# Large tiles moved to multiples of 512 bytes, and two modulation rounds summed on VectorE

## The chip, the cores and the metric

The kernel runs on 1 core of one Trainium2 chip. The metric is the device time of one execution in microseconds (us); the time before is the median of 3 runs. TensorE multiplies matrices, VectorE and ScalarE work elementwise, GpSimd (POOL in the profile) issues some small transfers, and SyncE (SP) issues the loads of the weights. Everything is float32; a product of two such matrices is made of three products in a reduced form of it (below).

## The reference

One sequence of 256 tokens with 1024 features passes through four layers: retention, forgetting attention, a convolution block with a dense feed-forward part, and a short convolution with a mixture of 8 experts. The first two are modulated by a vector c:

```python
c_act = jax.nn.silu(c)
for i in range(DEPTH):
    shift, scale, gate = jnp.split(c_act @ mod_w[i] + mod_b[i], 3, axis=-1)
    h = _rms_norm(x, norm_g[i]) * (1.0 + scale[:, None, :]) + shift[:, None, :]
    y = _retention(...) if i == 0 else _forgetting_attention(...)
    x = x + gate[:, None, :] * y
```

`mod_w` is 2 x 1024 x 3072: a vector times a matrix, of which only weight is large. In the last layer each token is sent to two of eight experts, and each expert has three matrices of 1024 x 3584:

```python
for e in range(N_EXPERTS):
    h = jax.nn.silu(x @ w_gate[e]) * (x @ w_up[e])
    out = out + gates[..., e:e + 1].astype(x.dtype) * (h @ w_down[e])
```

## The kernel before

All weights pass through one stream (class `Stream`, line 66) in units of 1 MiB: SP loads a unit into a raw buffer of 128 x 2048, ScalarE casts it into the high part wH (line 122), VectorE subtracts to get the low part wL (line 123), and TensorE multiplies with both (`mm3`, lines 229 to 233): high by high, high by low, low by high. There are three pairs of wH and wL, so a split runs at most two units ahead. In the retention there are three raw buffers; in the experts ten. `get` hands out the next unit and sends the loads and splits behind it on their way. Units of the modulation are not split: the raw buffer itself is read, and is given back once its reader is done.

The retention goes through four heads (`P_`, line 614): the products for q and k (weights stationary, 256 columns), then v and a gate (tokens stationary, 512 columns), with the attention of the head before (`A_`) in between. The modulation of layer 0's shift and scale is made in the start-up (line 1664). The rest is made in two rounds of eight steps in the heads: round 1 (the gates of both layers) in heads 0 and 1, round 2 (shift and scale of layer 1) in heads 2 and 3. `mods` (line 609) takes a step behind a projection, 2, 6, 4 and 4 times in the four heads. Step k multiplies 128 rows of `mod_w` by 128 values of c: four matmuls, each with one column of `sc` repeated 32 times as stationary side in its own quarter of the array's columns, add to one bank that is held through the round (line 499). `mod_end` (line 503) adds the bias.

The order of the work is made when the program is built: instructions are placed by priority (the order of the text) as their inputs become ready in its estimate, and each engine then works through its list in that order.

Where the tiles lie follows from their sizes. Pools are laid one behind the other, a tile is rounded up to 32 bytes per partition. In the program before, the small tiles of the pool `cp` leave the next large one (x) at byte 23680 of each partition, which is 46 x 512 + 128, and nearly everything behind it has sizes that are multiples of 512. So x, raw, wH, wL, hT, hH, hL, xn and the retention's and attention's outputs start at 128 past a multiple of 512. The statistics of the convolution block (192 bytes) put what follows in its pool (csg, cR, cW) at 320, and the router's rl, rmask and rpos (64 + 64 + 96 bytes) put what follows (oh, identR, three raw buffers, soH, soL, mh, xg, ohT, mhH, mhL) at 352. In the experts the gathered rows of expert e lie in xg where e is a multiple of 3, else in hT or hH (line 1329). ident, the first part of cst, lies at 416.

Of the kernel before, what the change touches and what calls it, by code (L numbers as in the profile page):

```python
# [6 lines left out]
F32 = mybir.dt.float32  # L7
# [3 lines left out]
ALU = mybir.AluOpType  # L11
# [3 lines left out]
P = 128  # L15
DM = 1024
# [9 lines left out]
C_STRIU, C_IOTA, C_TIE, C_ID32, C_MAIN = 146, 274, 530, 594, 626  # L26
# [166 lines left out]
class Kern:  # L193
# [4 lines left out]
    def t(self, pool, shape, tag, dt=F32, bufs=None):  # L198
        self.uid += 1
        kw = {} if bufs is None else {"bufs": bufs}  # L200
        return pool.tile(shape, dt, tag=tag, name=f"{tag}_{self.uid}", **kw)
# [228 lines left out]
    def setup(self, tmp):  # L430
        nc, a = self.nc, self.a
        cp = self.cp
        cv = cp.tile([P, 8], F32, name="cv")
        nc.scalar.dma_start(out=cv, in_=a["c"].rearrange("o (p k) -> p (o k)", k=8))
        self.x = self.t(self.xp, [P, 2, DM], "x", bufs=2)
        self.c = c = cp.tile([P, C_MAIN], F32, name="cst")
        nc.scalar.dma_start(out=c[:, 0:C_EARLY], in_=a["cst"][:, 0:C_EARLY])
        self.ident = c[:, C_ID:C_ID + P]
        vn = tmp.tile([32, P], F32, name="vn")
        nc.scalar.dma_start(out=vn[0:16, :], in_=a["norm_g"].rearrange("i d -> (i d)").rearrange("(k p) -> k p", p=P))  # L440
        nc.scalar.dma_start(out=vn[16:32, :], in_=a["mod_b"][0, 0:2 * DM].rearrange("(k p) -> k p", p=P))
        self.sc = cp.tile([P, 8], F32, name="sc")
        nc.scalar.activation(self.sc, cv, AF.Silu)
        self.ones = cp.tile([P, P], F32, name="ones")
        nc.gpsimd.memset(self.ones, 1.0)
        self.vr = [tmp.tile([P, P], F32, name=f"vr{i}") for i in range(2)]
        for r in self.vr:
            nc.gpsimd.memset(r, 1.0)
        self.wr = cp.tile([P, 8, N_EXP], F32, name="wr")
        ps = self.acc()  # L450
        nc.tensor.transpose(ps[:, 0:32], vn, self.ident[0:32, 0:32])
        self.vn = cp.tile([P, 32], F32, name="vnT")
        nc.vector.tensor_copy(self.vn[:, 0:24], ps[:, 0:24])
        nc.vector.tensor_scalar(self.vn[:, 24:32], ps[:, 24:32], 1.0, None, op0=ALU.add)
# [15 lines left out]
    def vectors(self):  # L470

        ps = self.acc()
        for i, r in enumerate(self.vr):
            self.nc.tensor.transpose(ps[:, i * P:(i + 1) * P], r, self.ident)
        self.v = self.cp.tile([P, 2 * P], F32, name="v")
        self.nc.vector.tensor_copy(self.v, ps[:, 0:2 * P])

    def vec(self, name):
        o = self.vcol[name]
# [6 lines left out]
    def mod_start(self, parts):  # L486

        b = self.t(self.bp, [P, 512], "mbias", bufs=1)
        for q, (i, n0) in enumerate(parts):
            self.nc.gpsimd.dma_start(out=b[32 * q:32 * (q + 1), :],  # L490
                                     in_=self.a["mod_b"][i, n0:n0 + 512].partition_broadcast(32))
        self.mps, self.mbias, self.mk = self.acc(), b, 0

    def mod_step(self):
        k = self.mk
        raw = self.st.get("mod")
        s = self.sc[:, k:k + 1].to_broadcast([P, 32])
        for q in range(4):
            self.nc.tensor.matmul(self.mps[32 * q:32 * (q + 1), :], s, raw[:, q * 512:(q + 1) * 512],
                                  start=(k == 0), stop=(k == 7), tile_position=(0, 32 * q))  # L500
        self.mk += 1

    def mod_end(self, tag):
        m = self.t(self.bp, [P, 512], tag, bufs=1)
        self.nc.vector.tensor_tensor(m, self.mps, self.mbias, op=ALU.add)
        return m

    def shift_scale(self, m, i):
# [243 lines left out]
    def fox(self):  # L752
        nc = self.nc
        fT, hH, hL = self.hT, self.hH, self.hL
        c = self.c
        with self.tc.tile_pool(name="fox", bufs=1) as fp:
# [82 lines left out]
                    nc.scalar.copy(v[:, tt, :], ps[tt])  # L839
                return v  # L840

            gq, gk = self.v[0:66, P + 24:P + 25], self.v[0:66, P + 25:P + 26]

            def stage_t(d):

# [87 lines left out]
            with self.soon():  # L933
                self.xo = self.t(self.xp, [P, 2, DM], "x", bufs=2)
                self.new_h(False)
                for tt in range(2):
                    r = self.residual(acc, grow, tt)
                    for nh in range(2):
                        xo = self.xo[:, tt, nh * 512:nh * 512 + 512]
                        if self.dbg:  # L940
                            self.dump_part("x2", xo, tt, nh)
                        nc.vector.scalar_tensor_tensor(xo, xo, r[:, 0:1], g[:, nh * 512:nh * 512 + 512],
                                                       op0=ALU.mult, op1=ALU.mult)
# [91 lines left out]
    def conformer(self):  # L1035
        nc = self.nc
        hH, hL = self.hH, self.hL
        with self.tc.tile_pool(name="conf", bufs=1) as cp:
# [4 lines left out]
            def glu(u):  # L1043
                sg = self.t(cp, [P, 512], "csg", bufs=2)

                def gate(ps):
                    nc.scalar.activation(sg, ps, AF.Sigmoid)
                    if u == 3:
                        self.table(AF.Silu, sg[:, 0:1])

                ps = self.proj_two("cg", "ca", u == 0, gate)
                if u == 0:
                    v = self.t(self.hp, [P, 2, DM], "xn", bufs=1)[:, :, 0:30 + T]
                    nc.gpsimd.memset(v[:, :, 0:30], 0.0)
                    nc.vector.tensor_tensor(v[:, :, 30:30 + T], sg.rearrange("p (c t) -> p c t", c=2),
                                            ps.rearrange("p (c t) -> p c t", c=2), op=ALU.mult)
                    return v
                nc.vector.tensor_tensor(sg, sg, ps, op=ALU.mult)
                R = self.t(cp, [P, 8 * (32 + T)], "cR", bufs=3).rearrange("p (q c t) -> p q c t", q=4, c=2)
                nc.gpsimd.memset(R[:, :, :, 0:36], 0.0)  # L1060
                sv = sg.rearrange("p (c t) -> p c t", c=2)
                for q in range(4):
                    for tau in range(4):
                        d, x = R[32 * tau:32 * (tau + 1), q, :, 32 + tau:32 + T], sv[32 * q:32 * (q + 1), :, 0:T - tau]
                        if q == tau:
                            nc.scalar.copy(d, x)
                        else:
                            (nc.gpsimd if (q + tau) % 2 else nc.sync).dma_start(out=d, in_=x)
                return R
# [26 lines left out]
                    turn(k)  # L1096
                stats(u)

            st = self.t(cp, [P, 2, 4, 6], "cst", bufs=1)

            def stats(u):
                for tt in range(2):
# [17 lines left out]
            v = glu(0)  # L1120
# [16 lines left out]
            with self.soon():  # L1137
                xn = self.t(self.hp, [P, 2, DM], "xn", bufs=1)
# [9 lines left out]
                for tt in range(2):  # L1148
                    nc.vector.tensor_scalar(xn[:, tt, 0:512], accT[tt][0], mv[:, tt, 0:1], r[:, tt:tt + 1],
                                            op0=ALU.subtract, op1=ALU.mult)  # L1150
# [37 lines left out]
    def short_conv(self):  # L1188
        nc = self.nc
        hH, hL = self.hH, self.hL  # L1190
        with self.tc.tile_pool(name="sc", bufs=1) as sp:
            oH = sp.tile([P, 8, T], F32R, name="soH")
            oL = sp.tile([P, 8, T], F32R, name="soL")
            wv = self.v[:, P:P + 24].rearrange("p (j k) -> p j k", j=3)
            xs = None
            v = lambda u: xs[:, u % 2 * 516:u % 2 * 516 + 516].rearrange("p (c t) -> p c t", c=2)
            for u in range(4):
                if u == 0:
                    def conv_in(ps):
                        nonlocal xs  # L1200
                        xs = self.t(self.hp, [P, 2, DM], "xn", bufs=1).rearrange("p a n -> p (a n)")
                        nc.gpsimd.memset(xs[:, 0:2 * 516], 0.0)
                        gate(ps)

                def gate(ps):
                    nc.scalar.copy(v(u)[:, :, 2:T + 2], ps.rearrange("p (c t) -> p c t", c=2))

                ps = self.proj_two("sc", "sh", u == 0, gate if u else conv_in)
                vu = v(u)
                nc.vector.tensor_tensor(vu[:, :, 2:T + 2], vu[:, :, 2:T + 2], ps.rearrange("p (c t) -> p c t", c=2), op=ALU.mult)  # L1210
                y = xs[:, 1032:1544].rearrange("p (c t) -> p c t", c=2)
                for ch in range(2):
                    k = 2 * u + ch
                    nc.vector.tensor_scalar(y[:, ch, :], vu[:, ch, 0:T], wv[:, 0, k:k + 1], None, op0=ALU.mult)
                    for j in (1, 2):
                        nc.vector.scalar_tensor_tensor(y[:, ch, :], vu[:, ch, j:j + T], wv[:, j, k:k + 1], y[:, ch, :],
                                                       op0=ALU.mult, op1=ALU.add)
                ps = self.proj_wst("sb", hH, hL)
                nc.vector.tensor_tensor(y, y, ps.rearrange("p (c t) -> p c t", c=2), op=ALU.mult)
                self.split_to(oH[:, 2 * u:2 * u + 2, :], oL[:, 2 * u:2 * u + 2, :], y, "dve")  # L1220
            return self.out_proj("so", oH, oL)


    def router_tiles(self, pool):
        t = lambda n, *sh: pool.tile([P, *sh], F32, name=n)
        self.rl = t("rl", 2, 8)
        self.rt = t("rmask", 2, 8), t("rpos", 3, 8)
        self.oh = self.t(pool, [P, 2, 2, P], "oh", F32R, bufs=1)

# [557 lines left out]
```

## Time and profile before

| | us |
|---|---|
| median of 3 runs (lowest to highest) | 1857.95 (1856.32 to 1862.34) |
| the profiled execution, its time | 1857.9 |
| the profiled execution, span of its instructions | 1856.1 |
| TensorE busy in the span | 1804.0 |
| VectorE busy | 1412.2 |
| ScalarE busy | 1063.9 |

The span runs from the first instruction to the last; busy time is a sum over very different stages, so the stages are read apart. The start-up takes the first 60 us, the retention goes on to about 260, the attention to about 450, the convolution block and its feed-forward part to about 710, the short convolution to about 830, and the experts to the end. PE is TensorE's multiplication and PEld its loading of the stationary side; DVE is VectorE, ACT ScalarE.

### The profile page before, as it was taken

Reading aid. Unit: us, or ns where it says so; the run is one execution under the profiler, and the core shown is the slowest. Engines: PE = TensorE matmul, PEld = TensorE weight load, DVE = VectorE, ACT = ScalarE, POOL = GpSimd, SP = SyncE. Lnnn points to the kernel's source line nnn. Section 1 sums busy time; section 2 is a strip of 40 time slices with the busy share of each in tenths; the row PEclk is TensorE's granted clock in tenths of the full one; section 3 lists DMA queues with packets and bytes.
Section 4 is the critical chain, followed back from the end, with each engine's and each line's share of the span. In section 5 each row is a group of like instructions: output and inputs, shape, how many; then the busy total and the mean of one; then the engine's idle time right before and its main releaser. Section 6 shows DMA issues by size and latency. Waiting matters only on the chain. (4 is left out here: it accounts for less than half of the span.)

```text
span 1856.1 us, 24359 instructions
## 1 busy us (share of the span) xinstructions
PE 1804.0 (97%) x9741; PEld 1485.4 (80%) x9741; DVE 1412.2 (76%) x1469; ACT 1063.9 (57%) x1036; POOL 65.7 (4%) x112
## 2 busy tenths in 40 slices
PE   6999999999999999999999999999999999999996
PEld 3867778788789998987888878878878888788785
DVE  2755656657875556778889888888888888888887
ACT  2333444664353333437777776767767767777674
POOL 1000002000200000000000000000000000000000
PEclk8999999999999999999999999999999999999998
DMA  9677636327546556647999999999999999999991
GB/s 358 213 263 270 216 125 207 114 86 240 159 134 199 189 182 204 228 159 260 351 367 348 354 339 349 374 351 357 338 346 364 375 353 347 341 356 363 362 360 74
DMA packets 252615, 509.34 MB, mean 274 GB/s; under 512 B 12347, under 2 KB 68782, under 8 KB 251470
## 3 DMA queue, kind: packets, MB, share of 16 engines
q1 hardware_dynamic: 249550, 500.64, 76.7%
q0 software_dynamic: 2592, 6.97, 1.2%
q8 instruction: 78, 1.28, 0.3%
q14 instruction: 43, 0.35, 0.1%
q10 hardware_dynamic: 352, 0.10, 0.0%
HBM read 504.28 MB, written 1.05 MB: 272 GB/s over the span
## 5 line engine op out<-in xcount | busy, mean ns | idle before, releaser
L123 DVE TENSOR_TENSOR wL<-raw,wH 128x2048 fp32r<-128x2048 f32 (+2 forms) x582 | 1032.3, 1800 | 229.3 <-ACT wH L122 227.9
L122 ACT CAST wH<-raw 128x2048 fp32r<-128x2048 f32 (+2 forms) x582 | 869.6, 1518 | 427.7 <-PE mm L232 118.2
L231 PE MATMUL mm<-hH,wH 128*128 128x256 f32 x816 | 232.2, 285 | 0.0
L232 PE MATMUL mm<-hL,wH 128*128 128x256 f32 x816 | 231.6, 284 | 0.0
L233 PE MATMUL mm<-hH,wL 128*128 128x256 f32 x816 | 231.2, 283 | 0.2 <-DVE wL L123 0.2
L231 PE MATMUL mm<-wH,hH 128*128 128x512 f32 (+1 forms) x512 | 200.1, 392 | 3.1 <-ACT wH L122 2.6
L232 PE MATMUL mm<-wL,hH 128*128 128x512 f32 (+1 forms) x512 | 199.6, 390 | 2.9 <-DVE wL L123 2.9
L232 PE MATMUL acc<-wL,mhH 128*128 128x512 f32 x448 | 179.1, 400 | 0.0
L233 PE MATMUL acc<-wH,mhL 128*128 128x512 f32 x448 | 176.6, 394 | 0.0
L231 PE MATMUL acc<-wH,mhH 128*128 128x512 f32 x448 | 164.4, 395 | 0.0
L231 PEld LDWEIGHTS mm<-hH,wH 128*128 128x128 f32 x816 | 156.5, 192 | 5.4 <-ACT wH L122 2.5
L233 PEld LDWEIGHTS mm<-hH,wL 128*128 128x128 f32 x816 | 156.5, 192 | 1.3 <-DVE wL L123 1.2
L232 PEld LDWEIGHTS mm<-hL,wH 128*128 128x128 f32 x816 | 156.5, 192 | 0.6 <-issue 0.2
L232 PE MATMUL mm<-wL,hT 128*128 128x512 f32 x336 | 131.9, 393 | 1.8 <-DVE wL L123 1.8
L232 PE MATMUL mm<-wL,xg 128*128 128x512 f32 x328 | 130.5, 398 | 1.3 <-DVE wL L123 1.2
L231 PE MATMUL mm<-wH,hT 128*128 128x512 f32 x336 | 131.5, 391 | 0.0
L233 PE MATMUL mm<-wH,hT 128*128 128x512 f32 x336 | 131.0, 390 | 0.0
L231 PE MATMUL mm<-wH,xg 128*128 128x512 f32 x328 | 130.2, 397 | 0.0
L233 PE MATMUL mm<-wH,xg 128*128 128x512 f32 x328 | 129.5, 395 | 0.0
L231 PEld LDWEIGHTS mm<-wH,hH 128*128 128x128 f32 x512 | 98.5, 193 | 28.5 <-ACT wH L122 4.5
L232 PEld LDWEIGHTS mm<-wL,hH 128*128 128x128 f32 x512 | 98.2, 192 | 25.0 <-DVE wL L123 6.4
L233 PE MATMUL mm<-wH,hL 128*128 128x512 f32 (+1 forms) x288 | 111.4, 387 | 0.7 <-DVE hL L361 0.7
(376 smaller groups left out, 2422.3 us busy)
## 6 DMA issues: line engine op xcount, KB each, us to landing
raw<-in_moe_w_gate_dram SPq DMA_DIRECT2D x112, 1024.0 KB
raw<-in_moe_w_up_dram SPq DMA_DIRECT2D x112, 1024.0 KB
raw<-in_moe_w_down_dram SPq DMA_DIRECT2D x111, 1024.0 KB
raw<-in_ret_w_in_dram SPq DMA_DIRECT2D x24, 1024.0 KB
raw<-in_mod_w_dram SPq DMA_DIRECT2D x32, 512.0 KB
raw<-in_fox_w_in_dram SPq DMA_DIRECT2D x16, 1024.0 KB
raw<-in_sc_w_in_dram SPq DMA_DIRECT2D x12, 1024.0 KB
raw<-in_ffn_w_gate_dram SPq DMA_DIRECT2D x11, 1024.0 KB
```

Of the source, the lines that this page charges most:

```text
L122: ops = (K.nc.scalar.copy(H[:, s], raw[:, s]), K.nc.vector.tensor_tensor(L[:, s], raw[:, s], H[:, s], op=ALU.subtract))
L123: K.nc.vector.tensor_tensor(L[:, s], raw[:, s], H[:, s], op=ALU.subtract))
L231: self.mm_first = mmul(ps, sH, mH, start=first, stop=False)
L232: mmul(ps, sH, mL, start=False, stop=False)
L233: self.mm_last = mmul(ps, sL, mH, start=False, stop=last)
```

## The change

Tiles are widened or narrowed so that the large ones move. In `cp`, cv takes 128 bytes for 32, cst 2560 for 2528, and v 256 for 1024, as only the 58 columns in use are kept (readers of v get the new column numbers). That is 640 bytes less, so x starts at 23040 = 45 x 512, and with it everything that was at 128 starts at a multiple of 512. The convolution block's statistics take 512 bytes for 192, and a tile rpad of 288 bytes fills up the router's 224, so that what was at 320 and 352 starts at a multiple of 512 too.

A step of the later modulation rounds is no longer four matmuls but one instruction of VectorE over 128 x 2048: the raw unit times one value per partition, in the first step written to a sum `msum`, in the others added to it. `msum` lies in the tile xn, which is free in the retention. `mod_end` sums over the partitions with four matmuls whose stationary side is ones, one per quarter, and then adds the bias as before. The bank is taken in `mod_end` and no longer at the start of the round. The start-up's modulation stays as it is.

```diff
     def setup(self, tmp):
-        cv = cp.tile([P, 8], F32, name="cv")
+        cv = cp.tile([P, 32], F32, name="cv")[:, 0:8]
...
-        self.c = c = cp.tile([P, C_MAIN], F32, name="cst")
+        self.c = c = cp.tile([P, 640], F32, name="cst")[:, 0:C_MAIN]
...
-        self.v = self.cp.tile([P, 2 * P], F32, name="v")
-        self.nc.vector.tensor_copy(self.v, ps[:, 0:2 * P])
+        self.v = self.cp.tile([P, 2 * P // 4], F32, name="v")
+        self.nc.vector.tensor_copy(self.v.rearrange("p (i n) -> p i n", i=2),
+                                   ps[:, 0:2 * P].rearrange("p (i n) -> p i n", i=2)[:, :, 0:32])
...
-        self.mps, self.mbias, self.mk = self.acc(), b, 0
+        self.mbias, self.mk = b, 0
+        self.msum = self.t(self.hp, [P, 2, DM], "xn", bufs=1).rearrange("p a n -> p (a n)")
 
     def mod_step(self):
         k = self.mk
         raw = self.st.get("mod")
-        s = self.sc[:, k:k + 1].to_broadcast([P, 32])
-        for q in range(4):
-            self.nc.tensor.matmul(self.mps[32 * q:32 * (q + 1), :], s, raw[:, q * 512:(q + 1) * 512],
-                                  start=(k == 0), stop=(k == 7), tile_position=(0, 32 * q))
+        w, o = self.sc[:, k:k + 1], self.msum
+        if k:
+            self.nc.vector.scalar_tensor_tensor(o, raw, w, o, op0=ALU.mult, op1=ALU.add)
+        else:
+            self.nc.vector.tensor_scalar(o, raw, w, None, op0=ALU.mult)
         self.mk += 1
 
     def mod_end(self, tag):
         m = self.t(self.bp, [P, 512], tag, bufs=1)
-        self.nc.vector.tensor_tensor(m, self.mps, self.mbias, op=ALU.add)
+        mps = self.acc()
+        for q in range(4):
+            self.nc.tensor.matmul(mps[32 * q:32 * (q + 1), :], self.ones[:, 0:32], self.msum[:, q * 512:(q + 1) * 512],
+                                  start=True, stop=True, tile_position=(0, 32 * q))
+        self.nc.vector.tensor_tensor(m, mps, self.mbias, op=ALU.add)
         return m
...
-            st = self.t(cp, [P, 2, 4, 6], "cst", bufs=1)
+            st = self.t(cp, [P, 128], "cst", bufs=1)[:, 0:48].rearrange("p (a b c) -> p a b c", a=2, b=4)
...
         self.rl = t("rl", 2, 8)
+        t("rpad", 72)
```

## Rows read from the trace of the kernel before

**Rows 1.** Busy time of each engine in four stretches, clock, DMA share, GB/s.
```profile
core 0: us, PE busy (x) PEld busy (x) DVE busy (x) ACT busy (x) POOL busy (x), PEclk, DMA share, GB/s
0.00:50.00 50.00, 33.75 (x205) 19.81 (x206) 16.46 (x35) 14.69 (x24) 7.38 (x19) 0.86 1.01 358
59.50:122.20 62.70, 62.70 (x376) 45.69 (x374) 38.72 (x64) 20.15 (x25) 1.11 (x2) 1.00 0.67 235
122.20:210.70 88.50, 87.78 (x494) 66.56 (x494) 54.07 (x72) 32.00 (x38) 4.24 (x8) 1.00 0.78 272
920.00:1820.00 900.00, 895.13 (x4030) 728.29 (x4029) 784.61 (x488) 645.34 (x457) 1.10 (x2) 1.00 0.98 352
```
**Rows 2.** Waits in 59.5 to 210.7 us: us in total, times, longest.
```profile
ACT wH L122 <- DMA raw<-in_ret_w_in_dram: 56.4, 12, 7.0
DVE wL L123 <- ACT wH L122: 40.0, 15, 6.4
...
PEld mm L231 <- ACT wH L122: 4.2, 5, 0.8
...
PEld mm L231 <- ACT roH L358: 1.7, 2, 0.8
```
**Rows 3.** Waits of SP's queue in the same stretch.
```profile
SPq L209 <- DVE wL L123: 48.8, 18, 4.6
SPq L209 <- PE acc L499: 45.8, 12, 5.8
```
**Rows 4.** Timeline of SP's queue in round 1: start, duration.
```profile
98.24 0.38 SPq L209 DMA_DIRECT2D raw<-in_ret_w_in_dram  x1
...
107.50 0.38 SPq L209 DMA_DIRECT2D raw<-in_ret_w_in_dram  x1
```
**Rows 5.** Timeline of TensorE around one modulation step.
```profile
65.16 0.28 PE L233 MATMUL mm<-hH,wL 128*128 128x256 f32 x1
65.36 1.06 PE L499 MATMUL acc<-raw,sc 128*32 128x512 f32 x8
...
66.58 0.28 PE L232 MATMUL mm<-hL,wH 128*128 128x256 f32 x1
```
**Rows 6.** Groups of instructions in 50 to 260 us: busy us, mean ns.
```profile
L499 PE MATMUL acc<-raw,sc 128*32 128x512 f32 x128 | 21.2, 604 | 0.0
```
**Rows 7.** Groups of VectorE's instructions in the whole span, by shape.
```profile
L123 DVE TENSOR_TENSOR wL<-raw,wH 128x2048 fp32r<-128x2048 f32 x320 | 725.2, 2288 | 76.9 <-ACT wH L122 75.7
L1378 DVE TENSOR_TENSOR mh<-mh,mm 128x512 f32<-128x512 f32 x56 | 38.4, 685 | 29.9 <-PE mm L233 29.0 <-ACT mh L1470 0.9
L1446 DVE SCALAR_TENSOR_TENSOR x<-mm,rgate,x 128x512 f32<-128x512 f32 x32 | 23.0, 746 | 9.4 <-PE mm L1438 9.4
L1696 DVE TENSOR_SCALAR xn<-x,rstd 128x1024 f32<-128x1024 f32 x2 | 1.5, 754 | 1.4 <-POOL rstd L369 1.4
L1529 DVE TENSOR_SCALAR x<-x 128x2048 f32<-128x2048 f32 x1 | 1.2, 1219 | 0.0
```
**Rows 8.** Timeline of TensorE, first and last of 12 matmuls of a down product.
```profile
892.63 0.39 PE L231 MATMUL acc<-wH,mhH 128*128 128x512 f32 x1
...
895.20 0.39 PE L233 MATMUL acc<-wH,mhL 128*128 128x512 f32 x1
```
**Rows 9.** Timeline of TensorE, first and last of 19 matmuls with xg.
```profile
896.80 0.39 PE L232 MATMUL mm<-wL,xg 128*128 128x512 f32 x1
...
901.00 0.39 PE L232 MATMUL mm<-wL,xg 128*128 128x512 f32 x1
```
**Rows 10.** Timeline of TensorE, first and last of 16 matmuls with hT.
```profile
1002.43 0.39 PE L233 MATMUL mm<-wH,hT 128*128 128x512 f32 x1
...
1005.83 0.39 PE L233 MATMUL mm<-wH,hT 128*128 128x512 f32 x1
```
**Rows 11.** Groups of TensorE's instructions from 820 us on.
```profile
L232 PE MATMUL acc<-wL,mhH 128*128 128x512 f32 x448 | 179.1, 400 | 0.0
...
L232 PE MATMUL mm<-wL,xg 128*128 128x512 f32 x328 | 130.5, 398 | 1.3 <-DVE wL L123 1.2
```
**Rows 12.** Waits in the experts, 820 to 1840 us.
```profile
ACT wH L122 <- PE mm L233: 98.4, 144, 1.5
...
PEld mm L232 <- DVE wL L123: 9.9, 13, 1.1
```

More of the change, by code (lines that the diff above doesn't have):

```diff
@@ L840, in vproj @@
                 return v
-            gq, gk = self.v[0:66, P + 24:P + 25], self.v[0:66, P + 25:P + 26]
+            gq, gk = self.v[0:66, 56:57], self.v[0:66, 57:58]
             def stage_t(d):
@@ L1193, in short_conv @@
             oL = sp.tile([P, 8, T], F32R, name="soL")
-            wv = self.v[:, P:P + 24].rearrange("p (j k) -> p j k", j=3)
+            wv = self.v[:, 32:56].rearrange("p (j k) -> p j k", j=3)
             xs = None
```

## The prediction

> **What bounds the kernel now.** I read the windows by stage first, because the change touches two stages that have different limits. [...] Busy alone does not say that TensorE is the limit, so the waits come next. In the retention the reader is to see that ScalarE waits for weights to land (56.4 us in 12 waits) and VectorE for ScalarE (40.0 us), while TensorE waits 4.2 us at most for any one of them [rows 2]: it is the limit, but its weights come just in time. Why just in time, the queue of the loads shows: SP waits 45.8 us in 12 waits for TensorE to finish a modulation step, as these hold two of the three raw buffers, and 48.8 us for the splits [rows 3]; weights are issued at 98.24 and again at 107.50 us [rows 4], 9.3 us for one unit. In the experts ScalarE waits for TensorE to give back split buffers (98.4 us in 144 waits), no wait for a DMA stands in that list, and TensorE waits 9.9 us for splits [rows 12]. So TensorE bounds the experts too, with the DMA close behind.
>
> **Part 1: alignment.** It adds no instruction to the stages. What it can change is how long one takes. The profile holds a natural experiment: the gathered rows xg of experts 0, 3 and 6 lie at 352 past a multiple of 512, the same rows of the other experts (in the tiles hT and hH) at 128; both are the stationary side, against the same moving wH and wL at 128. In xg the 19 starts from 896.80 to 901.00 us are 4.20/18 = 233 ns apart [rows 9]; in hT the 16 starts from 1002.43 to 1005.83 us 3.40/15 = 227 ns [rows 10]. The down products, stationary mhH and mhL at 352, go at (895.20 - 892.63)/11 = 234 ns [rows 8]. [...] I take 6.7 ns for each 512-column matmul whose stationary leaves the 352 place. There are 3 x 448 = 1344 in the down products and 3 x 328 = 984 with xg [rows 11]: 2328 x 6.7 = 15.6 us; 62 of the way back and 96 of the short convolution's output (by the code) add 1.1 us at the same price. All of it is on the engine that sets the end. What is late next: the loads, at share 0.98, and VectorE, which works 87%. If the supply ends at 352/0.98 = 359 GB/s, 2% of 900 us = 18 us can be won before it binds; the 50 us at the start, share 1.01 at 358 GB/s [rows 1], say 354 at a full share, which would allow 0.6% = 5.5 us. I take 14 us for the experts, near the first figure because ten raw buffers are filled when the stage begins, and 1 us for the rest. The other tiles go from 128 to 0, a place that no row shows: as 128 is the cheaper of the two seen, I take no change, with bounds of 4 ns per matmul either way.
>
> [...]
>
> **Part 2: the modulation sums.** Removed: 14 of 16 steps of TensorE. The 128 passes are 21.2 us busy [rows 6]; one step moves the next matmuls from 65.16 to 66.58 us, 1.42 us where two matmuls of 0.12 us would be 0.24 [rows 5], so 1.18 us per step, and some steps are cut in two by the schedule and pay twice. I take 21.2 us; the two bursts that stay cost 2 x 1.1: TensorE is relieved of 19 us, 9.5 per round.
> Added: per round one scalar product and seven products-and-sums of 128x2048 on VectorE. The first lies between 1.22 us (the same size with a constant) and 1.5 (twice the 0.754 of 128x1024 with a factor from memory), the others near the 2.29 us of the split subtraction of that size, plus the 0.06 by which the add with a factor from memory (0.746) exceeds a plain two-operand one (0.685 at 128x512): 2.35 [rows 7]. A round: 1.3 + 7 x 2.35 = 17.7 us.
> Round 1 (59.5 to 122.2): TensorE 62.7 - 9.5 = 53.2 us, VectorE 38.7 + 17.7 = 56.4 [rows 1]. VectorE is now the longer, so at most 6.3 us are won, and only if it never waits; it waits today 40 us over both rounds [rows 2]. I take 2. Round 2 (122.2 to 210.7): TensorE 88.5 - 9.5 = 79.0, VectorE 54.1 + 17.7 = 71.8, 91% of it; up to 9.5, I take 5. What helps: a modulation buffer is given back as soon as VectorE has added it, not when TensorE comes to that step, so SP's 45.8 us of waits go and two buffers serve the weights. What hurts: an add of 2.35 us standing ahead of a subtraction delays that split, and TensorE queues behind it, as do the rope products and the normalization of the head before. The closing matmuls wait for the last add; behind them in TensorE's queue stand the next head's projections, at worst 2.35 us twice. SP's queue is otherwise unmoved, POOL's keeps its bias loads. Bounds: a gain of 15.8 (6.3 + 9.5), a loss of 35.4 - 19 = 16.4 if every add lies on the path. The bank that each round no longer holds is worth at most the 1.7 us that TensorE waits for ScalarE's roH [rows 2]; taken as 0. The narrower copy of the vectors happens once, in the start-up, and is taken as 0.
>
> **The sum.** 2 + 5 + 14 + 1 = 22 us off the profiled execution's 1857.9 us (span 1856.1, 1.8 around it), which is the median of the runs (1857.95): 1836 us.
>
> **Rivals.**
> A. VectorE keeps what the retention wins. For it: 56.4 against 53.2 us in round 1. Against it: two more buffers for the weights. The retention then gives 0 instead of 7: 1843 us, and with the loss bound of 16.4 us, 1859.
> B. The place in memory is not the cause of the 6.7 ns (xg lies in another pool than hT). For it: no row shows place 0. Against it: mhH and xg are different tiles of one place and show the same 233 to 234 ns. Then only 7 us are won: 1851 us.
> C. The loads bind in the experts. For it: share 0.98, and 354 GB/s at the start. Against it: no engine waits for a landing there. The experts give 5.5 instead of 14: 1844 us. [...]
> D. Slower: place 0 is worse than 128, as 352 is. It would hit every matmul whose stationary lies at 128 today: by the page's and the code's counts some 3100 of 512 columns and 2450 of 256. At 6.7 ns that is 37 us, the 16.6 us of part 1 are not won, and 7 remain: 1888 us. It turns the kernel slower from (7 + 16.6)/5550 = 4 ns per matmul on. [...]
> E. Place 0 is better than 128 by up to 4 ns: 22 us more, 1814 us.
>
> **How the numbers follow.** About 0.3% (5.6 us) is what a measurement of this kernel tells from no change. Forecast (1827 to 1842): 0.54. A 0.13, of it 0.04 above 1852. B 0.08, half of it above 1852. C 0.11. D 0.06. E 0.08. Faster 0.54 + 0.09 + 0.04 + 0.11 + 0.08 = 0.86; same 0.04 + 0.04 = 0.08; slower 0.06. The range of 8 in 10 takes the forecast, C, most of A and half of E's way and of B: 1822 to 1851; unknown costs of a few us either way (the schedule is built anew) lie within it.
>
> **What would show it.** Right: the starts of the down products and of xg 227 ns apart as in hT; no modulation matmul in the retention but two bursts; round 1 shorter by 0 to 4 us and round 2 by 3 to 8; SP's waits for modulation steps gone; DMA share in the experts 0.99 or 1.00. Wrong: 233 ns still there (B); any stationary at 0 above 230 ns (D); ScalarE waiting for landings in the experts (C); TensorE waiting for wL by more than 5 us in round 1 (A).

## The result, and the profile after

The changed kernel takes 1824.89 us (median of 4 runs, 1823.88 to 1829.5) where the kernel before took 1857.13 beside it (1853.87 to 1862.34): a ratio of 0.983, 95% interval 0.980 to 0.986, so 32 us less. The forecast was 1836 (1822 to 1851): the time lies in the stated range, below the 1827 to 1842 that the forecast itself was given. The profiled execution of after took 1829.5 us; its span fell from 1856.1 to 1827.6, by 28.5.

The span can be cut at events of TensorE that both kernels have: the first product of q, the first of the attention's forget gate, the first of the router, the first gathered product of the experts, and the last product of the way back. Each entry is the time between two such starts in the timeline of the profiled execution, in us.

| kernel | start-up | retention | up to the router | routing | experts |
|---|---|---|---|---|---|
| before | 59.5 | 204.6 | 566.9 | 20.5 | 990.3 |
| after | 59.0 | 190.5 | 566.7 | 18.9 | 978.4 |
| align_only | 55.9 | 204.8 | 564.2 | 20.4 | 978.4 |
| mod_only | 56.6 | 189.6 | 567.3 | 20.4 | 990.3 |
| all_at_128 | 56.2 | 189.2 | 565.5 | 18.9 | 978.4 |
| all_at_352 | 59.3 | 191.3 | 566.1 | 18.9 | 978.4 |
| moving_at_32 | 57.0 | 192.8 | 572.3 | 20.4 | 1002.4 |
| steps_cut | 55.7 | 195.4 | 564.3 | 18.9 | 990.3 |
| changed_again | 58.3 | 189.9 | 565.1 | 18.9 | 978.4 |
| rope_early | 62.3 | 184.0 | 566.1 | 18.9 | 978.4 |
| rope_in_gap | 60.6 | 184.5 | 563.8 | 23.6 | 978.5 |

The first two lines say where the 28.5 us come from: 14.1 in the retention, 11.9 in the experts, 1.6 in the routing, under 1 elsewhere. The start-up's 4 us of spread belong to no edit: kernels with the same start-up have 56 and 59.

Busy time by stretch of after: round 1, round 2, and the middle of the experts.

```profile
core 0: us, PE busy (x) PEld busy (x) DVE busy (x) ACT busy (x) POOL busy (x), PEclk, DMA share, GB/s
59.00:114.60 55.60, 52.76 (x311) 46.29 (x310) 51.11 (x70) 19.82 (x24) 2.93 (x2) 0.94 0.74 248
114.60:195.20 80.60, 79.00 (x441) 65.24 (x443) 69.81 (x80) 32.25 (x38) 6.41 (x8) 1.00 0.88 310
905.00:1792.00 887.00, 881.48 (x4017) 726.56 (x4016) 782.46 (x487) 643.57 (x456) 1.10 (x2) 1.00 0.99 357
```

Against [rows 1], round 1 went from 62.7 to 55.6 us and round 2 from 88.5 to 80.6. TensorE's busy times, 52.8 and 79.0, lie at the sums of the forecast, 53.2 and 79.0, the first in part by chance: its granted clock in round 1 is 0.94, where it was 1.00. Where the same round ran at 1.00, in the kernel mod_only described below, TensorE was busy 50.4 us of it:

```profile
56.60:110.80 54.20, 50.36 (x311) 44.07 (x310) 50.67 (x70) 19.45 (x24) 2.94 (x2) 1.00 0.76 255
110.80:191.80 81.00, 78.97 (x437) 65.11 (x435) 70.11 (x80) 32.73 (x39) 6.42 (x8) 1.00 0.88 309
```

In after VectorE works 92% of round 1 instead of 62%, and the experts' loads move 357 GB/s instead of 352.

Waits of after in 59.5 to 200 us, then SP's own (us in total, times, longest), for [rows 2] and [rows 3]:

```profile
ACT wH L122 <- DMA raw<-in_ret_w_in_dram: 42.3, 10, 6.5
DVE wL L123 <- ACT wH L122: 13.6, 6, 5.4
...
PE mm L231 <- DVE t L613: 2.8, 1, 2.8
```
```profile
SPq L209 <- DVE wL L123: 59.8, 16, 8.4
SPq L209 <- DVE xn L502: 24.4, 9, 4.5
```

SP no longer waits for TensorE's modulation steps, but it waits 24.4 us for VectorE's adds (L502) instead of 45.8, and 59.8 for the splits instead of 48.8: the buffers come back earlier, not at once. VectorE's idle time behind ScalarE fell from 40.0 us to 13.6, so it took up most of the 35.4 us of adds. One wait is new, TensorE's 2.8 us. The added instructions (groups of VectorE in 50 to 260 us):

```profile
L502 DVE SCALAR_TENSOR_TENSOR xn<-raw,sc,xn 128x2048 f32<-128x2048 f32 x14 | 32.8, 2345 | 0.0
...
L504 DVE TENSOR_SCALAR xn<-raw,sc 128x2048 f32<-128x2048 f32 x2 | 2.6, 1282 | 0.0
```

They were put at 2.35 and 1.3 us. Last, one down product of 24 matmuls of after, first and last:

```profile
855.98 0.39 PE L231 MATMUL acc<-wH,mhH 128*128 128x512 f32 x1
...
861.20 0.39 PE L233 MATMUL acc<-wH,mhL 128*128 128x512 f32 x1
```

5.22/23 = 227.0 ns from start to start. A down product of the same 24 matmuls in before has 5.36/23 = 233.0, where the 12 of [rows 8] gave 234:

```profile
872.60 0.39 PE L231 MATMUL acc<-wH,mhH 128*128 128x512 f32 x1
...
877.96 0.39 PE L233 MATMUL acc<-wH,mhL 128*128 128x512 f32 x1
```

The gathered products of after take 393 ns each in the groups instead of 398 [rows 11]:

```profile
L232 PE MATMUL mm<-wL,xg 128*128 128x512 f32 x328 | 128.8, 393 | 1.8 <-DVE wL L123 1.7
```

### The profile page after: what moved, and what is told of

Its sections match the earlier page's. It is cut to its first block, busy times and chain, and to the rows that moved or that the text cites. A ratio compares the mean times of both kernels' runs of the same rounds, so it can differ in the third digit from the quotient of the medians.

```text
span 1827.6 us, 24165 instructions
## 1 busy us (share of the span) xinstructions
PE 1771.4 (97%) x9629; PEld 1484.3 (81%) x9629; DVE 1441.3 (79%) x1485; ACT 1064.7 (58%) x1036; POOL 69.7 (4%) x112
```

## The experiments

The theory after the comparison: the two parts are separate, the place of the stationary tile makes the experts' 11.9 us, and TensorE's relief the retention's 14. The rivals: one part needs the other; the loads or the buffers are behind it; it is not the place.

Each run stands beside runs of the kernel before, taken at the same time; where a ratio is given, it is to these.

**align_only**: the kernel before with the layout edits of the diff alone. **mod_only**: the kernel before with `mod_start`, `mod_step` and `mod_end` of the changed kernel alone.

> The kernel before with the layout edits alone (large tiles at 0 past a multiple of 512, modulation still summed by TensorE). Place theory: down products and xg start 227 ns apart instead of 233; the part from the short convolution on is shorter by what the changed kernel shows there (short convolution 0.5, routing 1.6, experts 12 us), the retention keeps its 151 us: 1843 to 1845 us, 13 to 15 faster than before. Rival, the gain in the experts comes from the new schedule behind part 2: then less than 5 us faster. Rival, the loads bind: 5 us.

> The kernel before with the modulation sums on VectorE alone (layout of before: large tiles at 128, xg and mh parts at 352). Theory from the changed kernel's trace: TensorE's relief reaches the end nearly whole, 14 to 15 us faster than before (1843), with the idle of 2.8 us in round 1 still there. The forecast's terms: 7 us (1851). Rival, the retention's gain needs the new place too: under 5 us.

Measured: 1840.12 us and 1840.20 against 1855.49 of before, ratios 0.992 (0.991 to 0.993) and 0.992 (0.990 to 0.993), 15.4 and 15.3 us faster. The table says where: align_only has the experts of after (978.4) and the retention of before (204.8), mod_only the other way round (990.3 and 189.6). The parts are separate. The retention gives 15.0 us without the layout, so the 7 of the forecast was too small by half. The routing's 1.6 us follow neither edit (20.4 in both, and 18.9 in steps_cut, which has the old layout). In before and in rope_in_gap, which have 20.5 and 23.6 us, a part of the routing ran at a granted clock of 0.66 and of 0.50, as the two stretches show; in after and in changed_again, which have 18.9, the clock stayed at 1.00 there. What lowers it was not tested.

```profile
838.00:843.00 5.00, 5.00 (x17) 3.96 (x17) 3.91 (x13) 5.00 (x6) 0.00 (x0) 0.66 0.54 162
```
```profile
815.00:820.00 5.00, 5.00 (x20) 4.61 (x21) 4.56 (x13) 4.16 (x5) 0.00 (x0) 0.50 0.46 143
```

**all_at_128** and **all_at_352**: the changed kernel with every large tile 128 and 352 bytes further on.

```diff
-        cv = cp.tile([P, 32], F32, name="cv")[:, 0:8]
+        cv = cp.tile([P, 64], F32, name="cv")[:, 0:8]     # all_at_352: 120
```

> The changed kernel with every large tile 128 bytes further on (at 128 past a multiple of 512). Theory, 0 and 128 are the same place for TensorE: the time of the changed kernel within 0.3% (1824 to 1830), all starts 227 to 228 ns apart. Rival, 0 is better than 128 by even 1 ns for some 5600 matmuls of 512 columns: 5 us or more slower.

> The changed kernel with every large tile at 352 past a multiple of 512. Theory, a stationary tile there costs 6 ns in each 512-column matmul: some 5600 of them by the trace's counts, 34 us slower than the changed kernel, and if the 2450 matmuls of 256 columns pay the same 15 more: 1859 to 1875 us, every start 233 ns apart. Rival, the price belongs to the expert pool's tiles and not to the place: only xg and the mh parts go back to 233 ns, 14 us slower (1839).

Measured: 1827.3 us (0.985 of before, 0.984 to 0.987) and 1826.63 (0.984, 0.983 to 0.986), both the time of the changed kernel. The second falls out of both theories: mhH now has the very address that it had in the kernel before, and costs nothing there. The down product of all_at_352:

```profile
856.55 0.39 PE L231 MATMUL acc<-wH,mhH 128*128 128x512 f32 x1
...
861.77 0.39 PE L233 MATMUL acc<-wH,mhL 128*128 128x512 f32 x1
```

So the place itself is not the cause. What before had and this kernel lacks is a distance: stationary at 352, moving weights at 128.

**places_mixed** and **moving_at_32** test the distance from either side: pads between the expert pool's tiles move the stationary ones away, or a pad of 32 bytes ahead of wH and one of 96 behind wL moves the weights.

```diff
+            self.t(mp, [P, 16], "pad1", bufs=1)          # places_mixed; pad2, pad3 likewise
             with self.soon(60):
                 xg[0], xg[1] = self.gather([0, 1], 0, self.oh, self.acc)
...
+                    K.t(K.wpool, [P, 8], "wpad", bufs=1)     # moving_at_32; wpad2 of 24 behind
```

> The changed kernel with three of the expert pool's stationary tiles moved away from the place of the moving weights (which stay at 0): xg and the one-hot parts at 64, mhH at 96, mhL at 256 past a multiple of 512; hT and hH stay at 0. Theory after the run with everything at 352: what costs is the distance between the stationary and the moving tile, not either's place. Then mhH starts 233 ns apart (96 past a multiple of 128, as 352 against 128 was), mhL 227, hT and hH 227, xg about 230 (64 past a multiple of 128, as the conformer's parts were in the kernel before); some 5 + 3 us slower than the changed kernel. Rival, the slow starts of before came from the raw buffers of the experts (at 352 there, at 0 here) or another neighbour: all stay at 227 to 228.

> The changed kernel with the split weights wH and wL at 32 and every other large tile at 128 past a multiple of 512: now the moving side is apart, by 96. Distance theory: every 512-column matmul whose stationary is not a weight goes at 233 ns, also hT, hH, the retention's and the feed-forward's; 5600 x 5.5 = 31 us slower than the changed kernel (1856), and up to 13 more if the 2450 matmuls of 256 columns, whose stationary is a weight, pay too. Rival, only the stationary's own place counts, and 128 is a good one: no change (1825).

Measured: 1836.12 us (one run) and 1859.42 (1.002 of before, 1.001 to 1.003), 32 us slower than all_at_128 and 35 slower than the changed kernel. In moving_at_32 x and the three raw buffers of the weights' own pool lie ahead of the pad, so at 0 and not at 128; the products shown read neither. The down product of places_mixed, then that of moving_at_32:

```profile
853.76 0.39 PE L231 MATMUL acc<-wH,mhH 128*128 128x512 f32 x1
...
859.04 0.40 PE L233 MATMUL acc<-wH,mhL 128*128 128x512 f32 x1
```
```profile
863.71 0.39 PE L238 MATMUL acc<-wH,mhH 128*128 128x512 f32 x1
...
869.10 0.40 PE L240 MATMUL acc<-wH,mhL 128*128 128x512 f32 x1
```

229.6 and 234.3 ns. With the weights moved, matmuls whose stationary tile stayed at 128, a good place in all_at_128, pay too. Groups of moving_at_32 from 820 us on:

```profile
L239 PE MATMUL mm<-wL,hT 128*128 128x512 f32 x336 | 134.0, 399 | 1.6 <-DVE wL L129 1.6
```

In after (groups from 806 us on) the same line is:

```profile
L232 PE MATMUL mm<-wL,hT 128*128 128x512 f32 x336 | 131.9, 392 | 2.0 <-DVE wL L123 1.9
```

So hT takes 399 ns where it took 392. The rival falls, and what costs lies between the two tiles. The 256-column matmuls, whose stationary side is a weight, pay nothing: 284 ns in moving_at_32 (200 to 800 us) as in after:

```profile
L239 PE MATMUL mm<-hL,wH 128*128 128x256 f32 x688 | 195.3, 284 | 0.0
```
```profile
L232 PE MATMUL mm<-hL,wH 128*128 128x256 f32 x688 | 195.4, 284 | 0.0
```

Two details missed. In places_mixed xg at 64 was put at 230 ns and took as much as in before (398 ns in the groups). And mhH at 96 was put at 233 ns and mhL at 256 at 227, two of the first to one of the second, which is 231 in the mean; 229.6 were measured, although moving_at_32, with the same 96 between its tiles, has 234.3. So the distance alone does not give the price. Which distances cost is asked by **places_32_256** and **places_128_192** (the same pads with other sizes):

> The changed kernel with xg and the one-hot parts at 32 and both mh parts at 256 past a multiple of 512, the moving weights at 0. If any distance that is not a multiple of 512 costs: xg 233 to 234 ns, mh parts 230 or more (in places_mixed mhH at 96 and mhL at 256 went at 230 both). If a multiple of 128 is enough: xg 233, mh parts 227 to 228.

> The changed kernel with xg and the one-hot parts at 128 and both mh parts at 192 past a multiple of 512, the moving weights at 0. If a multiple of 128 is enough: xg 227, mh parts 230 to 233. If any distance costs that is not a multiple of 512: both 230 to 234 ns.

Measured: 1830.8 and 1836.52 us, one run each, the experts 984.4 and 985.4 us. The two mh products, then xg's group, of places_32_256 and of places_128_192:

```profile
851.50 0.39 PE L231 MATMUL acc<-wH,mhH 128*128 128x512 f32 x1
...
856.71 0.39 PE L233 MATMUL acc<-wH,mhL 128*128 128x512 f32 x1
```
```profile
856.15 0.39 PE L231 MATMUL acc<-wH,mhH 128*128 128x512 f32 x1
...
861.41 0.39 PE L233 MATMUL acc<-wH,mhL 128*128 128x512 f32 x1
```
```profile
L232 PE MATMUL mm<-wL,xg 128*128 128x512 f32 x328 | 130.7, 398 | 1.3 <-DVE wL L123 1.3
```
```profile
L232 PE MATMUL mm<-wL,xg 128*128 128x512 f32 x328 | 130.5, 398 | 1.4 <-DVE wL L123 1.3
```

A distance of 256 costs nothing (5.21/23 = 226.5 ns) and 192 some 2 ns (228.7); 32 and 128 cost xg the full price, so the one expectation held for mh at 256 and the other for xg at 128; 228.7 at 192 is less than either gave. Free in these runs are 0 and 256, and of the other distances tried none is.

**steps_cut** takes TensorE's time of the steps away and leaves the buffers as they were:

```diff
+            n = 32 if k else 512
-            self.nc.tensor.matmul(self.mps[32 * q:32 * (q + 1), :], s, raw[:, q * 512:(q + 1) * 512],
+            self.nc.tensor.matmul(self.mps[32 * q:32 * (q + 1), 0:n], s, raw[:, q * 512:q * 512 + n],
```

> The kernel before with 14 of the 16 modulation steps cut from 512 to 32 columns on TensorE (the sums of the other columns are left out); VectorE gets nothing, and the raw buffers are still held until TensorE comes to the step. Theory, TensorE's time is what the retention won: 14 steps x about 1 us = 12 to 15 us faster than before, though SP's waits for the steps stay. Rival, the buffers given back early are what it won: under 5 us faster.

Measured: 1842.81 us against 1854.33, 0.994 (0.993 to 0.996), 11.5 us faster; the retention 9.3 us shorter. A cut step in TensorE's timeline:

```profile
68.29 0.28 PE L233 MATMUL mm<-hH,wL 128*128 128x256 f32 x1
68.50 0.27 PE L500 MATMUL acc<-raw,sc 128*32 128x32 f32 x8
68.69 0.39 PE L231 MATMUL mm<-hH,wH 128*128 128x256 f32 x1
68.92 0.28 PE L232 MATMUL mm<-hL,wH 128*128 128x256 f32 x1
```

From 68.29 to 68.92 are 0.63 us for a step and two matmuls of 0.12, so a cut step still costs 0.39 instead of 1.18, and 14 give 14 x 0.79 = 11.1 us, of which 9.3 reached the retention; the run's 11.5 hold the routing's 1.6 too, which belong to no edit. TensorE's time alone thus gives 9.3 of the retention's 14 to 15 us; the expected 12 to 15 left out the 0.39. The buffers have a part: SP's waits for the steps rose to 63.1 us, and TensorE now waits for late splits,

```profile
PE mm L231 <- ACT wH L122: 1.5, 2, 0.9
PE mm L233 <- DVE wL L123: 0.8, 1, 0.8
...
PE mm L232 <- DVE wL L123: 0.3, 1, 0.3
```

2.6 us in 55 to 200, which in after are 0.2 and 0.8 for the same splits. How much the early return is worth by itself was not run.

**rope_early** and **rope_in_gap** follow the new wait. TensorE's timeline of after, and three stretches around it:

```profile
81.91 0.28 PE L233 MATMUL mm<-hH,wL 128*128 128x256 f32 x1
85.03 0.77 PE L231 MATMUL mm<-wH,hH 128*128 128x512 f32 x1 [2.85 <-DVE t L613]
85.60 0.63 PE L232 MATMUL mm<-wL,hH 128*128 128x512 f32 x1
...
90.72 0.57 PE L232 MATMUL mm<-wL,hH 128*128 128x512 f32 x1
```
```profile
60.00:80.00 20.00, 20.00 (x169) 20.00 (x169) 18.93 (x26) 6.17 (x7) 0.00 (x0) 1.00 0.80 268
82.20:85.00 2.80, 0.00 (x0) 0.00 (x0) 2.80 (x6) 0.71 (x2) 0.00 (x0) 0.87 0.94 309
85.00:91.00 6.00, 5.97 (x14) 4.74 (x15) 6.00 (x7) 2.00 (x2) 0.00 (x0) 0.50 0.80 286
```

VectorE, 95% busy from 60 to 80 us with the adds, the splits and the rope tables, comes late to q's rope product (L613); TensorE stands still for 2.85 us, and then runs for 6 us at a granted clock of 0.50: its 13 starts from 85.60 to 90.72 us are 5.12/12 = 427 ns apart, where 512 columns took 227 ns in the down product of after. That costs some 3 us more (half of the 6). The tables, some 7 us of VectorE, depend on no weight, and VectorE is idle in much of the start-up: in after it is busy 22.4 of the first 59.0 us, 0.5 us of 16 to 23 and 0.4 of 34 to 42. rope_early computes them there at once; rope_in_gap behind the normalization of x (its call stands after `self.vector_rows()`).

```diff
-            CC, SS = self.rope_tables(r1, rp)
+            CC, SS = self.tables
...
                         self.setup(tp)
+                        self.tables = self.rope_tables(r1, tp)
```

> The changed kernel with the rope tables computed in the start-up, where VectorE is idle from 16 to 23 and from 34 to 42 us, instead of in round 1. Theory, TensorE's one wait of the retention (2.8 us for the first rope product) and the 6 us at half clock behind it are what VectorE's adds still cost: both go, 2.8 + 3 = 5 to 6 us faster than the changed kernel (1819). Rival, the adds hold TensorE in the same round at another place: 0 to 2 us. Rival, the start-up, which waits for its loads, becomes longer: slower.

> As rope_early, but the rope tables stand in the start-up behind the normalization of x on VectorE, in its idle stretch before the first modulation columns come (16 to 23 us), instead of ahead of it. Theory, what rope_early won in the retention (6.5 us: 184.0 us from the first projection of q to the forget gate instead of 190.5) stays, and its longer start-up (TensorE waits 4.8 us for the normalized x instead of 2.9) goes: 5 to 6 us faster than the changed kernel run beside it. Rival, the tables delay the first shift and scale, and the start-up gives back 2 us or more: 3 us or less.

> The changed kernel once more, on the chip of rope_in_gap, for a direct comparison: 1825 us, 0.983 of the kernel before.

rope_early: 1823.96 us, 0.984 of before (0.982 to 0.985), the time of the changed kernel and not the 5 to 6 us less that were expected. The retention is 6.5 us shorter and no wait of round 1 is left above 0.3, but the start-up is longer, as the last rival had it: the tables stand ahead of the normalization (L1711) on VectorE,

```profile
10.07 0.28 DVE L569 CAST t<-sT 128x256 f32<-128x256 int32 x1
...
18.12 0.75 DVE L1711 TENSOR_SCALAR xn<-x,rstd 128x1024 f32<-128x1024 f32 x1 [0.16 <-POOL rstd L369]
```

18.12 us instead of 14.06 in after. rope_in_gap: 1822.44 us (1821.24 to 1827.09), 0.983 (0.982 to 0.984), against 1826.83 (1822.2 to 1830.08), 0.985 (0.984 to 0.987), of the changed kernel beside it: 4.4 us less at the median, with intervals that touch, so that a gain is likely but not shown. Its rounds run at full clock:

```profile
60.50:113.00 52.50, 51.74 (x323) 44.52 (x323) 48.51 (x53) 19.61 (x23) 2.94 (x2) 1.00 0.87 289
113.00:192.40 79.40, 78.53 (x437) 65.25 (x437) 67.46 (x78) 33.45 (x40) 6.43 (x8) 1.00 0.89 306
```

In its retention 5.4 us are won (184.5 against 189.9); its profiled execution gives 4.7 back in the routing, at the low clock shown above, and its start-up, 60.6 us, is longer than in every kernel with the tables in the retention (59.5 at most).

## Why the prediction was right, and where not

- **The number: within the range, in part by luck.** The range reached down to 1822 for half of E's way, and E did not come; what brought the time there is above all that the retention gave 7 us more than the forecast's 7.
- **Part 1, 14 + 1 us: right in size, wrong in cause.** The experts gave 11.9 us, and in align_only as well. Per matmul that is 11.9/2328 = 5.1 ns. The 6.7 came from short stretches; within the unbroken product of 24 the price is 233.0 - 227.0 = 6.0, and a part of it goes into waits, as TensorE's loading waits 12.7 us for splits in the experts of after where it waited 9.9 [rows 12]. But the 352 place, which the step made the cause, costs nothing when the weights lie there too. Two groups that differed in the stationary place differed also in the distance to the weights, as the moving side never moved: the natural experiment had one variable more than it seemed. Rival B asked that question, and took the pool for the other variable.
- **D and E, place 0 against 128:** no difference (1827.3 against 1824.89 and 1826.83), as taken.
- **C:** the experts gave 11.9 us with the DMA at a share of 0.99, and ScalarE waited for no landing there, so the loads didn't bind. That no wait for a DMA stands in the list of waits is not exact, though: POOL waits 940.6 us for a landing in before and 927.8 in after.
- **Part 2, TensorE relieved by 19 us and VectorE loaded with 17.7 per round: right.** The prices are 2.345 and 1.282 us. TensorE's busy time in the two rounds fell from 150.5 us to 129.3 in mod_only, whose clock stayed at 1.00, and the closing burst of round 2 (1.06 us at 195.13 in after) lies behind them: some 20 us. Round 1 kept TensorE busy for 50.4 us and not 53.2; the burst that closes it, 1.1 of that sum, stands in round 2.
- **Part 2, 2 + 5 us kept: the term that was mis-sized.** It measured 14.1 (15.0 in mod_only): round 1 gave 7.1 of its 62.7 us, more than the 0 to 4 that were to show the forecast right, round 2 7.9 of its 88.5, and its closing burst behind it took back most of 1. The step that failed is "VectorE is now the longer, so at most 6.3 us are won" (mod_only won 8.5 in round 1, 62.7 to 54.2), with 2 and 5 taken in fear of its waits. VectorE's 56.4 us in round 1 were no floor, as after holds 51.1 there: the first product is done before the round (at 54.12 us), and 14 half splits lie in it instead of 15; the two make 2.5 us. Of the rest some is that instructions which follow one another without a pause overlap, so that a sum of their durations is too long; VectorE's timeline of after:

```profile
63.24 2.35 DVE L502 SCALAR_TENSOR_TENSOR xn<-raw,sc,xn 128x2048 f32<-128x2048 f32 x1
65.50 0.35 DVE L570 TENSOR_SCALAR t<-t,cst 128x256 f32<-128x256 f32 x1
```

  2.35 us of duration are 2.26 of time here. So TensorE remained the limit: round 2 is its 79.0 us and 1.6 more. A did not come either, as TensorE waited 0.8 us for wL in the retention, not 5. What VectorE kept was 2.8 us of idle TensorE and the 3 us at half clock behind it, at a place that the text named (the rope products) without a price.
- **"SP's 45.8 us of waits go":** about half, they are 24.4 us for the adds, and the waits for the splits grew by 11.0.

## What to carry to other kernels

Before a place in memory is blamed for a slow matmul, move both operands together and then each alone; in this kernel the 512-column matmuls whose stationary and moving tiles lie 0 or 256 bytes apart past a multiple of 512 went 2 to 7 ns faster than at the other distances tried. A sum of busy time bounds a whole chain, not a stretch of it: ask what of it can slide over the stretch's ends, and what the limiting engine has to do meanwhile. When work is moved onto an engine that idles late, look for what that engine does early in the stage and could have done before it: the rope tables cost 5.4 to 6.5 us in the retention, and VectorE has idle stretches in the start-up that hold them, though the start-up grew and the whole kernel won 4.4 us at the median.

## What was not expected of the hardware

- The start-to-start time of 512-column matmuls depends on where the stationary tile lies against the moving one: 226.5 to 227.0 ns at a distance of 0 and 256; 228.7 at 192; 229.6 with the high part at 96 and the low at 256; 233 at 224 and 234.3 with the weights at 32 (96 apart); xg at 32, 64 and 128 takes the long 398 ns of the groups. The 256-column ones with a weight as stationary side show nothing: 284 ns in the groups with the weights at 32 as with them at 0. Why 192 is between, why 128 is full, and why 96 costs less with the stationary tile moved than with the weights moved stays open.
- An idle TensorE of 2.85 us was followed by 6 us at a granted clock of 0.50 in after. In mod_only 3.0 us of idle at the same place left the clock at 1.00:

```profile
82.00:92.00 10.00, 8.51 (x38) 6.87 (x39) 10.00 (x12) 2.51 (x3) 0.00 (x0) 1.00 0.80 267
```

In changed_again 3.1 us of idle there were followed by 5 us at 0.69:

```profile
85.00:90.00 5.00, 5.00 (x17) 4.00 (x16) 5.00 (x7) 1.19 (x2) 0.00 (x0) 0.69 0.85 292
```

So the same wait can cost 3 us, 6, or something between, and the profile of one execution shows one of these.
